# A mixture of experts in a four-layer kernel: the gather between the first pair's products, slots counted by products, two more weight buffers, and six of eight combines done two by two

## The chip, the cores and the metric

The kernel runs on one core of a Trainium2 chip. The metric is the device time of one execution in microseconds (us). A core has five engines that work side by side: TensorE (PE in the profile; its weight loads are PEld), VectorE (DVE), ScalarE (ACT), GpSimd (POOL) and SyncE (SP), which here only issues DMA transfers. Each has its own instruction order and waits for the others by semaphores.

## The reference

Four layers over 256 latent tokens and 256 context tokens, 1024 channels. Each layer mixes the tokens in three recurrent branches and ends in an expert-choice mixture; the change is in that last part alone. Each of the 16 experts takes the 32 tokens of a stream with the highest probability for it, and its result is added to those tokens, weighted by that probability:

```python
def moe_ec(h, router_w, w1, w3, w2):
    B, n, _ = h.shape
    cap = max(1, CAP_FACTOR * n // N_EXPERTS)
    probs = jax.nn.softmax((h @ router_w).astype(jnp.float32), axis=-1)
    aff, idx = lax.top_k(jnp.swapaxes(probs, 1, 2), cap)
    bidx = jnp.arange(B)[:, None, None]
    xe = h[bidx, idx]
    hid = jax.nn.silu(jnp.einsum('becd,edf->becf', xe, w1)) * jnp.einsum('becd,edf->becf', xe, w3)
    ye = jnp.einsum('becf,efd->becd', hid, w2) * aff[..., None].astype(h.dtype)
    return jnp.zeros_like(h).at[bidx, idx].add(ye)
...
        x = x + mod_x[5][:, None] * moe_ec(h2x, router_w[l], moe_w1[l], moe_w3[l], moe_w2[l])
        if not last:
            ctx = ctx + mod_c[2][:, None] * merge_branches((a_c, b_c, m_c), gate_c, w_branch[l], w_out[l])
            h2c = modulate(rmsnorm(ctx, norm2_g[l]), mod_c[3], mod_c[4])
            ctx = ctx + mod_c[5][:, None] * moe_ec(h2c, router_w[l], moe_w1[l], moe_w3[l], moe_w2[l])
```

Layers 0 to 2 send both streams (512 tokens) through the experts, the last layer only the latent tokens. All weights of all experts are read in every layer, 402 MB in the whole kernel.

## The kernel before

**Route and slots.** The expert stage starts when the probabilities of the tokens stand as rows, one row for each expert and stream. Four rounds of max and match_replace mark the 32 chosen tokens (`sel`, 0 or 1). A scan on VectorE (L1599) counts them along a row, so that a chosen token gets its slot 1 to 32, and a multiplication (L1601) puts 0 at the others. Two transposes (L1604) turn this by token, and a comparison with 1 to 32 (L1614) makes `OH`, a 0/1 matrix from tokens to slots: for each of four tiles of 128 tokens, 16 experts x 32 slots.

**Gather.** `gather(eh)` multiplies the tokens, split into a high and a low part (`tok`), with `OH`: for each of eight channel tiles kk and each stream s, four products (L1630) into a bank `bi` (context) or `ai` (latent), then one eviction that applies scale and shift, on VectorE for the context stream (L1637), on ScalarE for the latent stream (L1635). `gather(0)` serves experts 0 to 7 and stands ahead of all expert products, `gather(1)` serves 8 to 15 and stands behind the w1 and w3 products of the first pair.

**Pairs.** The 16 experts go in eight pairs `pr_`. An expert has 64 slots, 32 of each stream, so that the two experts q = 0, 1 of a pair fill 128. For each pair: w1 products into `df` or `dm`, w3 products into the other (both L1650, 32 each: the two experts' products run side by side on the two 64-column halves of the array), SiLU on ScalarE and VectorE, four transposes (L1676) and a copy to `mrawf` (L1678), then 32 w2 products (L1684) into `ac` and `bi`. The **combine** brings the result back to the tokens: `Cm` holds which slot belongs to which token, from transposes (L1664) of `OH` times the probability, `aff` the probability of each slot. ScalarE scales and rounds (L1687, `mhif`), VectorE makes the rest (L1688, `mlof`), 16 products of 512 columns (L1694) follow, and VectorE adds each of them to the residual `xT` (L1697, two operations, one for each stream).

**Loads.** `Weights` hands out the expert weights: a load of 512 KB (tile `mw`) is half of the rows of w1, w3 or w2 that a step needs for one expert. A pair has 24 loads (8 of w1, 8 of w3, 8 of w2), a layer 192. They go through `N_MW` buffers:

```python
            i, l = self.n, self.l
            self.n += 1
            e, j = 2 * (i // 24) + i % 2, i % 24 // 2
            t = self.z.mt([1024], "mw", N_MW)
```

Four of these buffers hold another matrix (`ml`) until the products of the step ahead of the experts (w_out) are done. Loads for the first pair are asked for early, in `Weights.ahead`; the loop that calls it does so 16 times, fewer than `N_PRE`. SyncE issues all loads in order over eight semaphores, so that a load also waits for the eighth one before it to land.

**What sets the order.** A scheduler at build time orders the instructions of each engine by estimated times; so the combine of one pair is threaded into the w1 products of the next.

Of the kernel before, what the change touches and what calls it, by code (L numbers as in the profile page):

```python
# [30 lines left out]
def _consts():  # L31
# [47 lines left out]
N_MW = 22  # L79
# [27 lines left out]
N_PRE = 18  # L107
# [46 lines left out]
def tile_backbone(ctx: ExitStack, tc: tile.TileContext, A, out, dbg=None, depth=DEPTH):  # L154
# [1370 lines left out]
    def moe(z, l, P, last, rt, sums, W):  # L1525
# [92 lines left out]
        if last:  # L1618
            for xg in xe:
                gp.memset(xg[:, :, :, 0:32], 0.0)  # L1620

        def gather(eh):
            for kk in range(8):
                g, k = kk // 4, kk % 4
                for s in range(st0, 2):
# [6 lines left out]
                    o, pv = xe[g][:, k, 8 * eh:8 * eh + 8, 32 * s:32 * s + 32], ps.rearrange("p (e c) -> p e c", e=8)  # L1632
                    sc, sh = der[:, 1, kk, s:s + 1], mod[:, 24 + kk, s:s + 1]
                    if s:
                        se.activation(o, pv, AF.Identity, scale=sc, bias=sh)  # L1635
# [4 lines left out]
        for pr_ in range(8):  # L1640
            e0 = 2 * pr_
            ab = []
            for wn in ("w1", "w3"):
# [9 lines left out]
            if pr_ == 0:  # L1653
                gather(1)

            Ow = w2k("ada").rearrange("p (t e c) -> p t e c", t=4, e=2)
            gp.memset(Ow, 0.0)  # L1657
            for t in range(tl, 4):
                s = t // 2
                ve.tensor_tensor(Ow[:, t, :, 32 * s:32 * s + 32], OHf[:, t, e0 * 32:e0 * 32 + 64].rearrange("p (e c) -> p e c", e=2),  # L1660
                                 lg[:, t, e0:e0 + 2, None].to_broadcast([128, 2, 32]), ALU.mult)
# [102 lines left out]
```

## Time and profile before

| | |
|---|---|
| time, median of 3 runs | 5003.71 us (5001.26 to 5008.22) |
| the profiled execution | 5006.14 us, its span 5004.4 us |
| TensorE busy | 4513.4 us, 90% of the span |
| VectorE / ScalarE / GpSimd busy | 60% / 29% / 28% |
| data read from HBM | 795.81 MB |
| loads of expert weights | 768 of 512 KB |

In the trace the first w1 products of layers 0 to 3 start at 1056, 2326, 3601 and 4742 us, and the last pair's w2 products end near 1304, 2574, 3849 and 4980. A row of a timeline gives the start, the length, the engine, the line, the operation with its tiles (output <- inputs), how many instructions it holds, and in brackets the idle time before it and what ended it.

### The profile page before, as it was taken

What the parts mean: (1) busy time and instruction counts of PE and PEld (TensorE: products, weight loads), DVE (VectorE), ACT (ScalarE), POOL (GpSimd) and SP (SyncE); (2) the same over time, 40 slices, a digit from 0 to 9 for tenths busy, and PEclk for the clock granted to TensorE, in tenths of its full rate; (3) what the DMA queues carried; (4) which work ended last, traced back from release to release, by engine and by line L of the source; (5) the groups of instructions that cost most, each with busy time, mean ns of one, the idle gap of its engine ahead of it and who ended that gap; (6) DMA issues with size and microseconds to landing.
All of it is one profiled execution on the core that took longest, in us unless ns stands there. A gap on an engine that the chain in (4) does not pass through costs nothing.

```text
span 5004.4 us, 84862 instructions
## 1 busy us (share of the span) xinstructions
PE 4513.4 (90%) x31882; PEld 2934.2 (59%) x31882; DVE 2998.8 (60%) x8123; ACT 1470.0 (29%) x2932; POOL 1405.1 (28%) x1815
## 2 busy tenths in 40 slices
PE   7999999999889999989998999998998888887798
PEld 4666666653466666665336666666633666675533
DVE  4786757533477766663347777656333677776322
ACT  3333323220233332322023333332301433332211
POOL 3332323410243233232014333233300433332400
PEclk9999999999999999999999999999999899898899
DMA  5433446679532434457963244345697233333598
GB/s 219 119 112 110 119 148 202 234 262 393 214 106 65 126 106 125 156 191 257 394 258 110 63 119 112 101 150 167 234 390 289 77 83 84 86 88 107 198 392 315
DMA packets 684010, 886.03 MB, mean 177 GB/s; under 512 B 337072, under 2 KB 361264, under 8 KB 670800
## 3 DMA queue, kind: packets, MB, share of 16 engines
q1 hardware_dynamic: 683600, 880.60, 52.7%
q8 instruction: 252, 4.13, 0.3%
q14 instruction: 158, 1.29, 0.1%
HBM read 795.81 MB, written 84.63 MB: 176 GB/s over the span
## 4 chain that ended last, share of the span: by engine, by line
PE 50%; DVE 20%; DMA 6%; issue 4%; ACT 3%; POOL 2%; SPq 0%; DVEq 0%; ACTq 0%; POOLq 0%
PE df L393 9%; PE dm L393 8%; PE df L1650 5%; PE ai L211 5%; PE bi L211 5%; PE dm L1650 4%; PE bi L1694 3%; PE ac L211 2%; PE ac L1684 2%; PE bi L1684 2%; DMA t<-gates 2%; DVE cv L1037 2%; DMA mw<-in_w_dram 1%; DVE sv L428 1%; POOL wlo L367 1%
## 5 line engine op out<-in xcount | busy, mean ns | idle before, releaser
L367 POOL TENSOR_TENSOR wlo<-wraw,whi 128x512 fp32r<-128x512 f32 x696 | 942.6, 1359 | 1934.3 <-ACT whi L366 1708.0
L393 PE MATMUL df<-big,whi 128*128 128x512 f32 (+1 forms) x2944 | 892.0, 384 | 0.0
L393 PE MATMUL dm<-big,whi 128*128 128x512 f32 (+1 forms) x2368 | 740.1, 392 | 1.1 <-DVE big L367 1.1
L393 PE MATMUL df<-big,wlo 128*128 128x512 f32 (+1 forms) x1536 | 650.8, 424 | 70.3 <-POOL wlo L367 23.2
L366 ACT CAST whi<-wraw 128x512 fp32r<-128x512 f32 x696 | 426.5, 617 | 870.6 <-PE df L393 442.4
L393 PEld LDWEIGHTS df<-big,whi 128*128 128x128 f32 x2944 | 567.5, 201 | 90.8 <-issue 3.7
L393 PE MATMUL dm<-big,wlo 128*128 128x512 f32 (+1 forms) x1248 | 528.5, 424 | 57.0 <-POOL wlo L367 18.6
L393 PEld LDWEIGHTS dm<-big,whi 128*128 128x128 f32 x2368 | 458.9, 198 | 85.4 <-DVE big L367 2.8
L393 PEld LDWEIGHTS df<-big,wlo 128*128 128x128 f32 x1536 | 306.7, 200 | 197.0 <-issue 97.1
L393 PEld LDWEIGHTS dm<-big,wlo 128*128 128x128 f32 x1248 | 247.1, 198 | 164.9 <-issue 71.9
L1650 PE MATMUL df<-mw,big 128*64 128x512 f32 x1024 | 302.2, 610 | 0.0
L1037 DVE SCALAR_TENSOR_TENSOR cv<-cv,par,cv 128x255 f32<-128x255 f32 (+3 forms) x472 | 249.0, 539 | 42.6 <-ACT cv L1034 38.8
L1697 DVE SCALAR_TENSOR_TENSOR big<-bi,der,big 128x256 f32<-128x256 f32 x448 | 191.8, 478 | 120.3 <-PE bi L1694 119.9
L1650 PE MATMUL dm<-mw,big 128*64 128x512 f32 x1024 | 255.7, 594 | 2.1 <-DMA mw<-in_w_dram 1.9
L1657 POOL MEMSET mada<- 128x512 f32 x32 | 16.8, 525 | 800.7 <-PE bi L1694 350.4
L722 DVE SCALAR_TENSOR_TENSOR big<-cv,muc,big 128x252 f32<-128x252 f32 (+2 forms) x280 | 156.6, 581 | 33.2 <-ACT big L719 31.8
L1650 PEld LDWEIGHTS dm<-mw,big 128*64 128x64 f32 x1024 | 80.8, 137 | 152.5 <-issue 136.7
L1688 DVE SCALAR_TENSOR_TENSOR mlof<-ac,aff,mhif 128x512 fp32r<-128x512 f32 x32 | 24.0, 750 | 212.3 <-ACT mhif L1687 212.3
L211 PE MATMUL ai<-AR,BK 64*128 64x128 f32 (+1 forms) x1024 | 124.0, 320 | 29.8 <-POOL BK L905 12.3
L1684 PE MATMUL ac<-mw,mrawf 128*64 128x512 f32 x512 | 139.6, 600 | 9.9 <-ACT mrawf L1678 9.9
L1694 PEld LDWEIGHTS bi<-mada,mhif 128*128 128x128 f32 x256 | 48.0, 187 | 155.1 <-issue 82.7
L1684 PE MATMUL bi<-mw,mrawf 128*64 128x512 f32 x512 | 138.1, 592 | 0.0
(514 smaller groups left out, 7871.8 us busy)
## 6 DMA issues: line engine op xcount, KB each, us to landing
mw<-in_w_dram SPq DMA_DIRECT2D x768, 512.0 KB, 10.4
wraw<-in_w_in_dram SPq DMA_DIRECT2D x536, 256.0 KB, 2.8
adaw<-in_ada_w_dram SPq DMA_DIRECT2D x96, 1024.0 KB, 6.3
gates<-gt SPq DMA_DIRECT2D x114, 256.0 KB, 3.4
wraw<-in_w_branch_dram SPq DMA_DIRECT2D x96, 256.0 KB, 2.7
t<-gates SPq DMA_DIRECT2D x85, 256.0 KB, 3.7
TU<-zoai SPq DMA_DIRECT2D x128, 128.0 KB, 3.1
wraw<-in_w_out_dram SPq DMA_DIRECT2D x64, 256.0 KB, 5.1
```

What stands on the lines that cost most here:

```text
L211: mm(o, a, b, **kw)
L366: se.copy(dst_hi, src)
L367: eng.tensor_tensor(dst_lo, src, dst_hi.bitcast(F32), ALU.subtract)
L393: mm(ps[:, c0:c1], a[:, k % 4, :], bk[:, c0:c1], start=(n == 0), stop=(n == 3 * nk - 1))
L428: ve.tensor_tensor(tv, Xb[:, j + 1:, j:j + 1].to_broadcast(sh), Xb[:, j:j + 1, 0:j].to_broadcast(sh), ALU.mult)
L722: ve.scalar_tensor_tensor(dst, src, muc[:, 1 + q, rb:rb + 1], dst, ALU.mult, ALU.add)
L1037: ve.scalar_tensor_tensor(dst, src, cw[:, cb, t:t + 1], dst, ALU.mult, ALU.add)
L1650: mm(ps[64 * q:64 * q + 64, :], xe[k // 4][:, k % 4, e0 + q, :], wt[q][:, k2 * 512:(k2 + 1) * 512], start=(k == 0), stop=(k == 7))
L1684: mm(py[hf][64 * q:64 * q + 64, :], hT[:, kk, 64 * q:64 * q + 64], wt[q][:, hf * 512:(hf + 1) * 512], start=(kk == 0), stop=(kk == 3))
L1688: ve.scalar_tensor_tensor(yl[hf], py[hf], aff, yh[hf].bitcast(F32), ALU.mult, ALU.subtract)
L1694: mm(pcb[:, n], y[db // 4][:, db % 4 * 128:(db % 4 + 1) * 128], Cm[:, n], start=y is yh, stop=y is yl)
L1697: ve.scalar_tensor_tensor(xT[:, db, cs_], pcb[:, cs_], der[:, 3, db, s:s + 1], xT[:, db, cs_], ALU.mult, ALU.add)
```

## The change

Four things change, in `route_begin`'s expert part and in two constants.

1. The slots: `sel` is transposed first, and the count along the tokens is made by three products with a triangular matrix (`mf_0`) and a matrix of ones.
2. `gather(0)` is cut: channel tiles 0 and 1 ahead of the first product, the others between the steps of the first pair's w1 products. An eviction becomes two, each for every other pair, because the place of the streams in a pair's 64 slots now depends on the pair's parity (`s ^ r_`).
3. `N_MW` 22 becomes 24, `N_PRE` 18 becomes 20.
4. Pairs 0 to 5 are combined two by two. With the streams swapped in odd pairs, a tile of 128 rows can hold one stream of two pairs: after an even pair four copies, each masked to one stream by `af`, put its w2 products into `ys`; after an odd pair four operations add its own. `ys` is then split into a high part (ScalarE) and a low part (VectorE for one half of the channels, GpSimd for the other), and one combine of 32 products of 256 columns serves both pairs. Pairs 6 and 7 are combined alone, as before.

```diff
-N_MW = 22
+N_MW = 24
...
-        sel, slot = z.mt([256], "sel"), z.mt([256], "slot")
-        ve.tensor_scalar(sel[lp], wk[lp], -1.0, None, ALU.is_equal)
-        ve.tensor_tensor_scan(slot[lp], C["ones"][lp, 0:1].to_broadcast([64 - 32 * st0, 256]), sel[lp], 0.0, ALU.mult, ALU.add)
-
-        ve.tensor_tensor(slot[lp], slot[lp], sel[lp], ALU.mult)
+        ve.tensor_scalar(wk[lp], wk[lp], -1.0, None, ALU.is_equal)
...
+        ve.tensor_copy(sel[:, :, sv], pst[:, 0:128].rearrange("p (q e) -> p q e", q=2)[:, :, sv])
+
+        pst = z.psm()
+        mm(pst[:, 32 * st0:64], C["mf_0"], sel[:, 0, sv], start=True, stop=True)
+        mm(pst[:, 64 + 32 * st0:128], C["ones"], sel[:, 0, sv], start=True, stop=False)
+        mm(pst[:, 64 + 32 * st0:128], C["mf_0"], sel[:, 1, sv], start=False, stop=True)
+        ve.tensor_tensor(stm[:, :, sv], pst[:, 0:128].rearrange("p (q e) -> p q e", q=2)[:, :, sv], sel[:, :, sv], ALU.mult)
...
-        gather(0)
+                    for r_ in range(2):
+                        o = xv[:, :, r_, :, 32 * (s ^ r_):32 * (s ^ r_) + 32]
+                        if s:
+                            se.activation(o, pv[:, :, r_], AF.Identity, scale=sc, bias=sh)
+                        else:
+                            ve.tensor_scalar(o, pv[:, :, r_], sc, sh, ALU.mult, ALU.add)
+        gather(0, range(2))
...
+                    if pr_ == 0 and wn == "w1" and kk < 3:
+                        gather(0, range(2 * kk + 2, 2 * kk + 4))
                     wt = [W.take() for q in range(2)]
...
+            if r_ == 0:
+                ys = [[w2k("rawm") for hf in range(2)], [z.mt([512], "ys", 2) for hf in range(2)]]
             for hf in range(2):
-                se.activation(yh[hf], py[hf], AF.Copy, scale=aff)
-                ve.scalar_tensor_tensor(yl[hf], py[hf], aff, yh[hf].bitcast(F32), ALU.mult, ALU.subtract)
...
+                for s in range(st0, 2):
+                    if r_ == 0:
+                        se.activation(ys[s][hf], py[hf], AF.Copy, scale=af[:, 0, s:s + 1])
+                    else:
+                        ve.scalar_tensor_tensor(ys[s][hf], py[hf], af[:, 1, s:s + 1], ys[s][hf], ALU.mult, ALU.add)
+            if r_ == 0:
+                continue
+            yh, yl = [[[w2k(x + f, F32R) for _ in range(2)] for f in "fm"] for x in ("hi", "lo")]
+            for hf in range(2):
+                for s in range(st0, 2):
+                    split(yh[s][hf], yl[s][hf], ys[s][hf], (ve, gp)[hf])
             for db in range(8):
                 pcb = psum("bi")
-                for y in (yh, yl):
-                    mm(pcb[:, n], y[db // 4][:, db % 4 * 128:(db % 4 + 1) * 128], Cm[:, n], start=y is yh, stop=y is yl)
                 for s in range(st0, 2):
                     cs_ = slice(s * 256, (s + 1) * 256)
+                    for y in (yh, yl):
+                        mm(pcb[:, cs_], y[s][db // 4][:, db % 4 * 128:(db % 4 + 1) * 128], Cm[:, cs_], start=y is yh, stop=y is yl)
```

TensorE's order in layer 0 before, at the end of `gather(0)` (L1630; `ai` is the bank, `OH` and the parts of a token tile the inputs) and the first w1 products (L1650, into `df`, `mw` the weights, `big` the gathered tokens):

```order
L1630 MATMUL ai_10598<-OH_10497,mada_10460 128x256
L1630 MATMUL ai_10598<-OH_10497,mada_10461 128x256
L1630 MATMUL ai_10598<-OH_10497,ssq_10471 128x256
L1630 MATMUL ai_10598<-OH_10497,gt_10472 128x256
L1650 MATMUL df_10604<-mw_9996,big_10506 64x512
L1650 MATMUL df_10604<-mw_9998,big_10506 64x512
L1650 MATMUL df_10604<-mw_9996,big_10506 64x512
L1650 MATMUL df_10604<-mw_9998,big_10506 64x512
```

After the change, where the gather is L1634 and the expert products L1660:

```order
L1634 MATMUL ai_10546<-OH_10499,mhim_10416 128x256
L1634 MATMUL ai_10546<-OH_10499,mlom_10417 128x256
L1634 MATMUL ai_10546<-OH_10499,mhif_10427 128x256
L1634 MATMUL ai_10546<-OH_10499,mlof_10428 128x256
L1660 MATMUL df_10538<-mw_9996,big_10508 64x512
L1634 MATMUL bi_10539<-OH_10499,mhim_10394 128x256
L1634 MATMUL bi_10539<-OH_10499,mlom_10395 128x256
L1634 MATMUL bi_10539<-OH_10499,mhif_10405 128x256
L1634 MATMUL bi_10539<-OH_10499,mlof_10406 128x256
L1634 MATMUL bi_10553<-OH_10499,mhim_10394 128x256
L1634 MATMUL bi_10553<-OH_10499,mlom_10395 128x256
```

The first product now stands behind the gather of the first channel tiles and stands alone; the gather of the next ones follows it, and the other products of its step come behind that.

TensorE's order in layer 0 before, where the w2 products of pair 2 (L1684) end and its combine (L1694) meets pair 3's w1 products:

```order
L1684 MATMUL bi_11112<-mw_11137,mrawf_11109 64x512
L1684 MATMUL ac_11111<-mw_11139,mrawf_11109 64x512
L1684 MATMUL bi_11112<-mw_11139,mrawf_11109 64x512
L1664 MATMUL ai_11265<-cst,mada_11259 128x128
L1694 MATMUL bi_11153<-mada_11095,mhif_11145 128x512
L1650 MATMUL df_11193<-mw_11194,big_10506 64x512
L1694 MATMUL bi_11153<-mada_11095,mlof_11147 128x512
L1694 MATMUL bi_11158<-mada_11095,mhif_11145 128x512
L1694 MATMUL bi_11158<-mada_11095,mlof_11147 128x512
L1650 MATMUL df_11193<-mw_11196,big_10506 64x512
L1650 MATMUL df_11193<-mw_11194,big_10506 64x512
```

After the change, at the same place (w2 products L1715), no combine follows:

```order
L1715 MATMUL ac_11134<-mw_11160,mrawf_11132 64x512
L1715 MATMUL ac_11134<-mw_11162,mrawf_11132 64x512
L1715 MATMUL bi_11135<-mw_11160,mrawf_11132 64x512
L1715 MATMUL bi_11135<-mw_11162,mrawf_11132 64x512
L1660 MATMUL df_11176<-mw_11177,big_10508 64x512
L1660 MATMUL df_11176<-mw_11179,big_10508 64x512
L1660 MATMUL df_11176<-mw_11177,big_10508 64x512
L1660 MATMUL df_11176<-mw_11179,big_10508 64x512
L1660 MATMUL df_11176<-mw_11185,big_10508 64x512
L1660 MATMUL df_11176<-mw_11187,big_10508 64x512
```

The w1 products of pair 3 stand in one block, two halves side by side. Behind pair 1 the combine of pairs 0 and 1 (L1753) is threaded into pair 2's w1 products after the change:

```order
L1715 MATMUL bi_10924<-mw_10949,mrawf_10921 64x512
L1715 MATMUL bi_10924<-mw_10951,mrawf_10921 64x512
L1660 MATMUL df_11033<-mw_11036,big_10508 64x512
L1660 MATMUL df_11033<-mw_11042,big_10508 64x512
L1753 MATMUL bi_10977<-mada_10782,mhif_10961 128x256
L1660 MATMUL df_11033<-mw_11044,big_10508 64x512
L1660 MATMUL df_11033<-mw_11042,big_10508 64x512
L1660 MATMUL df_11033<-mw_11044,big_10508 64x512
L1660 MATMUL df_11033<-mw_11050,big_10509 64x512
L1753 MATMUL bi_10984<-mada_10782,mhif_10961 128x256
L1753 MATMUL bi_10977<-mada_10782,mlof_10965 128x256
```

Six w1 products stand ahead of the first product with a low part (`mlof`).

SyncE's order in layer 0 before the change, with the waits of each issue, where the w2 loads of pair 0 (L1492) meet pair 1's w1 loads (L1490); `DMAHW` is the landing of an earlier load, `PE` a buffer that TensorE frees, and adaw (and wraw, later in the stage) are loads of the next layer's other weights:

```order
L1492 DMA mw_10763<-in_w_dram 128x1024 [waits DMAHW2_49]
L1492 DMA mw_10765<-in_w_dram 128x1024 [waits DMAHW3_49]
L1492 DMA mw_10771<-in_w_dram 128x1024 [waits DMAHW4_49,PE_49]
L1492 DMA mw_10773<-in_w_dram 128x1024 [waits DMAHW5_49,PE_49]
L1492 DMA mw_10779<-in_w_dram 128x1024 [waits DMAHW6_49,PE_49]
L1492 DMA mw_10781<-in_w_dram 128x1024 [waits DMAHW7_49,DVE_49,PE_49]
L306 DMA adaw_13612<-in_ada_w_dram 128x2048 [waits DMAHW0_49,PE_49]
L1492 DMA mw_10787<-in_w_dram 128x1024 [waits DMAHW1_49,PE_49]
L1492 DMA mw_10789<-in_w_dram 128x1024 [waits DMAHW2_49,PE_49]
L1490 DMA mw_10844<-in_w_dram 128x2x512 [waits DMAHW3_49,PE_49]
```

After the change (L1493, L1491, adaw L307):

```order
L1493 DMA mw_10805<-in_w_dram 128x1024 [waits DMAHW2_49]
L1493 DMA mw_10807<-in_w_dram 128x1024 [waits DMAHW3_49]
L1493 DMA mw_10813<-in_w_dram 128x1024 [waits DMAHW4_49]
L1493 DMA mw_10815<-in_w_dram 128x1024 [waits DMAHW5_49]
L1493 DMA mw_10821<-in_w_dram 128x1024 [waits DMAHW6_49,PE_49]
L1493 DMA mw_10823<-in_w_dram 128x1024 [waits DMAHW7_49,PE_49]
L1493 DMA mw_10829<-in_w_dram 128x1024 [waits DMAHW0_49,PE_49]
L1493 DMA mw_10831<-in_w_dram 128x1024 [waits DMAHW1_49,DVE_49,PE_49]
L307 DMA adaw_13589<-in_ada_w_dram 128x2048 [waits DMAHW2_49,PE_49]
L1491 DMA mw_10846<-in_w_dram 128x2x512 [waits DMAHW3_49,PE_49]
```

Four loads instead of two go out without a wait for TensorE, and all eight w2 loads stand ahead of the adaw load.

## Rows read from the trace of the kernel before

**Rows 1.** Page, 40 slices: GB/s moved, slice by slice.

```profile
GB/s 219 119 112 110 119 148 202 234 262 393 214 106 65 126 106 125 156 191 257 394 258 110 63 119 112 101 150 167 234 390 289 77 83 84 86 88 107 198 392 315
```

**Rows 2.** Windows view: stretch, length, busy by engine, PEclk, DMA share, GB/s.

```profile
core 0: us, PE busy (x) PEld busy (x) DVE busy (x) ACT busy (x) POOL busy (x), PEclk, DMA share, GB/s
...
1080.00:1099.40 19.40, 19.40 (x80) 6.33 (x80) 9.17 (x23) 1.90 (x3) 0.12 (x1) 1.00 0.94 355
1161.25:1192.97 31.72, 29.89 (x123) 10.55 (x121) 11.44 (x26) 2.45 (x4) 0.53 (x1) 1.00 1.04 394
4800.00:4880.00 80.00, 74.75 (x336) 27.83 (x334) 22.39 (x48) 7.46 (x12) 1.58 (x3) 1.00 1.04 395
```

**Rows 3.** Timeline of SyncE's DMA issues, layer 0 and layer 3: start, length, count.

```profile
1058.10 0.80 SPq L1492 DMA_DIRECT2D mw<-in_w_dram  x2
...
1271.36 9.78 SPq L1492 DMA_DIRECT2D mw<-in_w_dram  x8
1282.10 1.62 SPq L374 DMA_DIRECT2D wraw<-in_w_in_dram  x2
...
4958.77 9.78 SPq L1492 DMA_DIRECT2D mw<-in_w_dram  x8
```

**Rows 4.** Page, DMA issues: count, KB each, us to landing.

```profile
mw<-in_w_dram SPq DMA_DIRECT2D x768, 512.0 KB, 10.4
```

**Rows 5.** Timeline of TensorE, end of layer 0's w2 products, then layer 3's.

```profile
1303.62 1.08 PE L1684 MATMUL bi<-mw,mrawf 128*64 128x512 f32 x4
...
4968.20 1.93 PE L1650 MATMUL dm<-mw,big 128*64 128x512 f32 x6 [0.26 <-DMA mw<-in_w_dram]
...
4978.73 0.59 PE L1684 MATMUL bi<-mw,mrawf 128*64 128x512 f32 x1
```

**Rows 6.** Timeline of TensorE, one steady pair of layer 0 [idle before].

```profile
1192.97 7.45 PE L1650 MATMUL dm<-mw,big 128*64 128x512 f32 x31
...
1210.44 0.50 PE L1694 MATMUL bi<-mada,mhif 128*128 128x512 f32 x1 [0.76 <-ACT mhif L1687]
1210.87 1.07 PE L1650 MATMUL df<-mw,big 128*64 128x512 f32 x2
...
1224.64 1.88 PE L1650 MATMUL dm<-mw,big 128*64 128x512 f32 x7
```

**Rows 7.** Timeline of TensorE, layer 0, between pairs 0 and 1.

```profile
1087.74 0.50 PE L1694 MATMUL bi<-mada,mhif 128*128 128x512 f32 x1
...
1099.39 7.45 PE L1650 MATMUL dm<-mw,big 128*64 128x512 f32 x31
```

**Rows 8.** Timeline of VectorE, layer 0, from the selection to the slots.

```profile
1040.43 1.63 DVE L1599 TENSOR_TENSOR_SCAN slot<-cst,sel 64x256 f32<-64x256 f32 x1
1042.10 1.30 DVE L1601 TENSOR_TENSOR slot<-slot,sel 64x256 f32<-64x256 f32 x1
1043.97 0.29 DVE L1607 COPY stm<-ai 128x128 f32<-128x128 f32 x1 [0.57 <-PE ai L1604]
```

**Rows 9.** Timeline of TensorE, layer 0: first gather, w1 and w2 products.

```profile
1044.87 0.58 PE L1630 MATMUL bi<-OH,mhim 128*128 128x256 f32 x1 [0.94 <-DVE OH L1614]
...
1056.14 7.09 PE L1650 MATMUL df<-mw,big 128*64 128x512 f32 x32
...
1080.74 1.03 PE L1684 MATMUL ac<-mw,mrawf 128*64 128x512 f32 x4
```

**Rows 10.** Groups by line: count, min/median/max ns, first and last start.

```profile
L1635 ACT ACTIVATE big<-ai,mod,der x64: 562/565/567, 1047.6 to 4768.6; 128x256 f32<-128x256 f32 x64
...
L1687 ACT ACTIVATE mhif<-ac,aff x32: 687/688/689, 1087.0 to 4979.5; 128x512 fp32r<-128x512 f32 x32
...
L1688 DVE SCALAR_TENSOR_TENSOR mlof<-ac,aff,mhif x32: 741/751/752, 1087.7 to 4980.2; 128x512 fp32r<-128x512 f32 x32
```

**Rows 11.** Windows view, layer 0: first and later gather products.

```profile
1044.80:1049.40 4.60, 4.53 (x20) 4.34 (x20) 3.36 (x10) 1.13 (x2) 0.00 (x0) 0.50 0.00 0
1050.70:1056.10 5.40, 5.40 (x45) 5.27 (x44) 2.97 (x6) 2.26 (x4) 0.00 (x0) 1.00 0.00 0
```

More of the change, by code (lines that the diff above doesn't have):

```diff
@@ L106 @@
 AM0, AMS = 800.0, 0.0
-N_PRE = 18
+N_PRE = 20
 AD, AD0 = 180.0, 30.0
@@ L1619, in moe, with gather @@
             for xg in xe:
-                gp.memset(xg[:, :, :, 0:32], 0.0)
-        def gather(eh):
-            for kk in range(8):
+                for r_ in range(2):
+                    gp.memset(xg.rearrange("p k (a r q) c -> p k a r q c", r=2, q=2)[:, :, :, r_, :, 32 * r_:32 * r_ + 32], 0.0)
+        def gather(eh, kks):
+            for kk in kks:
                 g, k = kk // 4, kk % 4
@@ L1653, in moe @@
             if pr_ == 0:
[L1654 to L1661, printed above, removed]
-            pc = z.psm()
-            for t in range(tl, 4):
-                te.transpose(pc[:, t * 128:(t + 1) * 128], Ow[:, t].rearrange("p e c -> p (e c)"), ident)
@@ new lines, in moe @@
+            if pr_ >= 6:
+                yh, yl = [w2k("hif", F32R) for _ in range(2)], [w2k("lof", F32R) for _ in range(2)]
+                for hf in range(2):
+                    se.activation(yh[hf], py[hf], AF.Copy, scale=aff[:, 0:1])
+                    ve.scalar_tensor_tensor(yl[hf], py[hf], aff[:, 0:1], yh[hf].bitcast(F32), ALU.mult, ALU.subtract)
+                if pr_ == 7:
+                    X["ss"] = psum("dm")
+                for db in range(8):
+                    pcb = psum("bi")
+                    for y in (yh, yl):
+                        mm(pcb[:, n], y[db // 4][:, db % 4 * 128:(db % 4 + 1) * 128], Cm[:, n], start=y is yh, stop=y is yl)
+                    for s in range(st0, 2):
+                        cs_ = slice(s * 256, (s + 1) * 256)
+                        ve.scalar_tensor_tensor(xT[:, db, cs_], pcb[:, cs_], der[:, 3, db, s:s + 1], xT[:, db, cs_], ALU.mult, ALU.add)
+                    if pr_ == 7:
+                        sums.add_all(db, xT[:, db], X["ss"])
+                continue
@@ new lines, in moe @@
+            if r_ == 0:
+                ys = [[w2k("rawm") for hf in range(2)], [z.mt([512], "ys", 2) for hf in range(2)]]
+            for hf in range(2):
+                for s in range(st0, 2):
+                    if r_ == 0:
[3 more added lines that the diff above has]
+            if r_ == 0:
+                continue
```

63 lines of the change are left out of this document (45 added, 18 removed).

## Prediction

> **What bounds the kernel now.** I read the 40 slices of the page first. The data rate stands at 390 or more in four places, one for each layer [rows 1]: these are the expert stages, and the change touches nothing else. So the question is what bounds an expert stage. The windows of the second view [rows 2] say that the sixteen DMA engines are full there: from pair 1 on the share is 1.04 at 394 GB/s, in layer 0 (one full pair stands for the four like it) and in layer 3. A load of 524,288 B then takes 524,288 / 394,000 = 1.33 us, and a pair's 24 loads 31.9 us, as long as a pair takes on TensorE (dm to dm, 1192.97 to 1224.64, 31.67 us [rows 6]). The two run at one pace because a load waits for a buffer that TensorE frees.
>
> Which of them would give way? In layers 0 to 2 the loads lie ahead. A layer has 768 / 4 = 192 [rows 4]. SyncE issues 170 of them (192 less the 22 buffers) after the first products have freed a buffer, the first at 1058.10, the last at 1271.36 + 9.78 = 1281.1 [rows 3]; with the median landing of 10.4 us [rows 4] the last one lands near 1291.5, and near 1289 if the queue is shorter by then. The group of w2 products that uses it starts at 1303.62 [rows 5]; four products are two side-by-side pairs of 0.43 (below), so w2 ends at 1304.5. The loads are 12 us ahead: in these layers TensorE ends last. In layer 3, with half the tokens, it is the other way round: TensorE stops for a load in the last pair's w3 products (idle 0.26, ended by DMA [rows 5]), and the last w2 products at 4978.73 come with the last landing, 4968.5 + 10.4 [rows 3 to 5]. Layer 3 is bound by the loads already.
>
> **Combine of six pairs two by two.** Now every pair's combine (16 products of 512 columns) is threaded into the next pair's w1 products. Alone, 32 products take 7.45 less a tail of 0.57, 6.88 us, since two 64-column halves run side by side, 0.43 a pair (the first row of [rows 6]). With the combine between them it takes from 1210.44 to 1224.64, 14.20 us, after an idle 0.76; a side-by-side pair that is broken up costs about 1.0 (1.07 for two records [rows 6]). So a pair boundary without a combine saves 14.20 + 0.76 - 6.88 = 8.1 us. It is gone after pairs 0, 2 and 4. After pair 0 the stretch is 1087.74 to 1099.39 [rows 7], 11.65 us with 26 products left, 26 x 0.215 = 5.6: 6.05 saved. Sum 6.05 + 2 x 8.1 = 22.2 us for each of layers 0 to 2. The combine after pairs 1, 3 and 5 has 32 products of 256 columns, the columns of one old combine, so it keeps its price.
>
> What it adds: on ScalarE four copies like L1687 (0.69 [rows 10]) after an even pair. They free the two accumulators that TensorE needs only at the next w2 products, over 13 us later: hidden. After an odd pair VectorE runs four operations like L1688 (0.75 [rows 10], 3.0 us), and the splits come on top, before a low half can be multiplied; now it is one copy and one such operation. Behind the waiting product stand w1 products on TensorE. The order after pair 1 puts six of them ahead of the first low half, which cover most of the wait. Bounds: 0 (all covered) and 3.0 us (nothing covered); I take 0.8, nearer the first, since the first two w1 products stand alone at about 1.0 each. Left: 22.2 - 2.4 = 19.8 us. TensorE alone would end the layer's w2 products at 1304.5 - 19.8 = 1284.7.
>
> **Slots counted by products.** The scan (1.63) and the multiplication (1.30) with a 0.04 gap go: 2.97 us [rows 8]. In their place come three small products and a multiplication out of PSUM; nearest is the copy that stands there now, 0.29 with 0.57 of waiting for TensorE before it [rows 8], and I allow 0.5 for the products: 1.35. Saved 1.6 us; bounds 0.5 and 2.5.
>
> **Gather between the first products.** Nothing is removed: the same gather products stand before and between the first w1 products, so the first of these moves from 1056.14 to about 1048.5, and w3 hardly moves. The order breaks up one or two side-by-side pairs (0.6 each), and every switch costs a bit: +1.5 us, bounds 0 and 3. The evictions become twice as many with half the elements; one of 256 takes 0.565 [rows 10], so two halves take at most 1.13 beside eight gather products of 0.12 (0.96 us [rows 11]): hidden but for the bound just given. So the first w2 products, 1080.74 now [rows 9], stay where they are within 1.5 us.
>
> What the earlier products could give is earlier loads: the first buffer comes free some 5 us before 1058.10. But w1 and w3 of pair 0 free only 16 buffers, and the next ones come with the w2 products at 1080.74; 16 loads need 16 x 1.33 = 21 us, which 1058.1 already leaves. The head start is spent waiting in the second gather, ahead of the w2 products.
>
> **Two more buffers.** All 24 loads of pair 0 are then issued before its first product (on SyncE the two extra ones pass ahead of an adaw load). At 1080.74 two more loads are done, 2 x 1.33 = 2.7 us for the end of the loads. The rate is 355 GB/s in 1080 to 1099 against 394 later [rows 2]: 19.4 x (1 - 355/394) = 1.9 us that unbroken w1 products, which free buffers faster, may give back.
>
> **The sum.** In layers 0 to 2 the loads now end last. They end at 1291.5 - 2.7 = 1288.8 (at best 1289 - 2.7 - 1.9 = 1284.4). The last two buffers serve two groups of products, 1.7 us more: 1290.5 (1286). The gain is 1304.5 - 1290.5 = 14.0, up to 18.5; I take 15, nearer the first since the 10.4 is measured. TensorE's own bound (19.8) lies 5 us beyond. Three layers: 45. Layer 3, where the loads end last already, gains the 2.7 and about the 1.6 of the slots, since its first pair starts earlier by that: 4.2. Together 49: 5006.1 (the profiled execution, 1.7 over its span) - 49 = 4957. The median of the three runs is 2.4 lower: **4955 us**. Its own range: 12 to 18.5 a layer and 3 to 5 for layer 3, so 39 to 60 us: 4944 to 4965.
>
> **Rivals.** A, the loads don't bind: if buffers come free sooner and the queue never runs dry, TensorE's 19.8 to 22.2 is gained in full, 59 to 67 + 4: 4933 to 4940, about 4938. For it: the bound at best (18.5) is near. Against: the share is 1.04 already, and no window has more than 395. Chance 0.12.
>
> B, the longer chain after odd pairs is in the open: at the bound of 3.0 us or more, with the splits on GpSimd late for the second half, each of the three combines loses 3 to 5 us, so that 22.2 shrinks to 7 to 13 a layer and TensorE stays last. 21 to 39 + 4: 4961 to 4979, about 4970. For it: the idle 0.76 of today comes from a chain of a single copy. Against: w1 products are there to fill it. Chance 0.14.
>
> C, slower: TensorE's clock falls. After waits like the 0.94 before the first gather product [rows 9] it was granted 0.50, the lower of its two levels (1.2 GHz), and 20 gather products took 4.60 us; at 1.00 (2.4 GHz) 45 took 5.40 [rows 11]. The change makes TensorE wait for loads in pairs 5 to 7. A pair without waits is 3 x 6.88 + 3 = 23.6 us; at the lower level about 45, which is 13 over the 31.9 of its loads. Three such pairs in four layers are +156, less the 49: 5110. It ends slower from somewhat over one such pair a layer (15 / 13). Against: layer 3 waits for loads today, and its window shows 1.00 with TensorE busy 74.75 of 80 us [rows 2]. Chance 0.04.
> The Trainium skill (TensorE: Matmul & The Clock Gate, HAM oscillation) tells of a kernel whose clock falls in each wait for a transfer. The rows of layer 3 show such waits without it.
>
> D, the loads bind already: if a load took longer than 1.33 us, the end of the loads would be the end of the layer today, and only the 2.7 a layer and the 1.6 of layer 3 would be gained, 12 us: 4991. Against: 394 and 395 GB/s [rows 2] and the 12 us by which the last load is early. Chance 0.01.
> The Trainium skill (DMA: Bandwidth & Descriptors, Where 436 GB/s comes from) has transfers from HBM bound by a core's share of it, about 358 GB/s. An estimate by that page is 1.46 us a load, and 154 loads from 1080 would end at 1305; the trace disagrees in every full pair.
>
> E, no change: what follows takes the gain back. The next layer's first weights go out right behind the last expert load, at 1282.10 now [rows 3], 22 us before the w2 products end; that lead falls to about 11. Chance 0.04.
>
> **How the numbers follow.** Forecast 0.65 (4944 to 4965), A 0.12, B 0.14, C 0.04, D 0.01, E 0.04. The range 4938 to 4978 takes in nearly all of B and the edge of A. 0.2% is 10 us, about what a measurement of this kernel tells from no change. Faster by more than that: forecast, A, B and D, 0.92; within 0.04 (E); slower 0.04 (C).
>
> **What would show it.** Right: the w1 products after pairs 0, 2 and 4 in one block of 7 us; waits for loads on TensorE in pairs 5 to 7 of layers 0 to 2, at a clock of 1.00; a DMA share of 1.04 from pair 1 to the last load; the first product of layer 0 near 1048.5 and its first w2 products near 1081; the last group of w2 products near 1289. Wrong: no wait for loads at the end (A), TensorE idle for over 3 us at the combine after odd pairs (B), a clock under 1 in the pairs (C), the last expert load as late as now (D).

## Result and the profile after

The changed kernel takes 4949.97 us (median of four runs, 4939.53 to 4968.46), the kernel before 5005.8 us beside it: ratio 0.9894, 95% interval 0.9863 to 0.9924. It is faster, by some 53 us (1.1%) by the ratio and 56 by the two medians; 4955 us was forecast. The profiled execution took 4948.79 us, its span is 4946.3 us.

The single execution is a blunt measure: the changed kernel's runs differ by 29 us. The expert stages, read between two fixed instructions, are not. From the start of the first gather product to the end of the last w2 product, in us by layer, and the distance from the end of the last expert load's issue in layer 0 to the end of its w2 products:

| kernel | layer 0 | layer 1 | layer 2 | layer 3 | last issue to end, layer 0 |
|---|---|---|---|---|---|
| before | 259.8 | 259.9 | 258.2 | 241.1 | 23.6 |
| after | 245.6 | 244.5 | 244.7 | 238.6 | 11.8 |
| difference | -14.3 | -15.4 | -13.6 | -2.5 | |

In the kernel before, layer 3 alone had a distance of 11.8: the last issue row of [rows 3] ends at 4968.55, the last w2 products at 4979.29 + 1.02 = 4980.31.

```profile
4979.29 1.02 PE L1684 MATMUL bi<-mw,mrawf 128*64 128x512 f32 x2
```

In layer 0 before, TensorE hardly waited for an expert load (waits view, 1060 to 1304 us: in all 0.7 us, twice, 0.4 the longest):

```profile
PEld df L1650 <- DMA mw<-in_w_dram: 0.7, 2, 0.4
```

The page's slices still have one hump of the data rate for each layer, as [rows 1]:

```profile
GB/s 218 122 102 113 126 138 194 217 268 394 259 110 63 118 115 117 163 174 264 394 292 111 66 119 112 107 151 162 246 382 302 86 79 88 84 88 107 213 392 310
```

The windows view after the change (columns as [rows 2]) shows the same saturation from pair 1 on, in front of it a stretch with a share of 0.74, and a clock of 1.00 in all three; the first gather products ahead of them still ran at 0.50:

```profile
1047.00:1052.00 5.00, 4.45 (x20) 4.33 (x20) 4.17 (x13) 1.44 (x4) 0.00 (x0) 0.50 0.00 0
1084.00:1090.00 6.00, 6.00 (x30) 2.01 (x28) 1.76 (x13) 0.00 (x0) 0.00 (x0) 1.00 0.74 258
1100.00:1182.00 82.00, 77.85 (x366) 29.83 (x364) 31.57 (x73) 10.31 (x17) 7.09 (x5) 1.00 1.04 392
1182.00:1290.00 108.00, 99.42 (x418) 36.95 (x415) 28.50 (x56) 10.89 (x18) 3.81 (x3) 1.00 1.04 395
```

TensorE's timeline after, layer 0: the first gather product (L1634), the first w1 product (L1660), the first w2 products (L1715), pair 3's w1 products, the three waits in the combine behind pair 3 (L1753), waits for loads in pair 5's w3 products, and the end:

```profile
1047.55 0.58 PE L1634 MATMUL bi<-OH,mhim 128*128 128x256 f32 x1 [0.84 <-DVE OH L1617]
...
1052.31 1.10 PE L1660 MATMUL df<-mw,big 128*64 128x512 f32 x2
...
1084.03 1.03 PE L1715 MATMUL ac<-mw,mrawf 128*64 128x512 f32 x4
...
1143.32 7.04 PE L1660 MATMUL df<-mw,big 128*64 128x512 f32 x32
...
1168.05 0.38 PE L1753 MATMUL bi<-mada,mhif 128*128 128x256 f32 x1 [0.75 <-ACT mhif L367]
...
1169.98 0.39 PE L1753 MATMUL bi<-mada,mlof 128*128 128x256 f32 x1 [0.53 <-DVE mlof L368]
...
1171.66 0.39 PE L1753 MATMUL bi<-mada,mlom 128*128 128x256 f32 x1 [0.95 <-DVE mlom L368]
...
1208.95 2.43 PE L1660 MATMUL dm<-mw,big 128*64 128x512 f32 x8 [0.22 <-DMA mw<-in_w_dram]
1211.66 2.44 PE L1660 MATMUL dm<-mw,big 128*64 128x512 f32 x8 [0.28 <-DMA mw<-in_w_dram]
1214.37 2.43 PE L1660 MATMUL dm<-mw,big 128*64 128x512 f32 x8 [0.27 <-DMA mw<-in_w_dram]
...
1292.10 1.02 PE L1715 MATMUL bi<-mw,mrawf 128*64 128x512 f32 x2
```

The block of w1 products in 7.04 us is what the combine used to break up: [rows 6] had 14.20 us there. The kernel's loops issue 16 products for a pair's w1, and the trace counts 32: it has two records for each, so the counts of 32 for w1, w3 and w2 are counts of records, x4 is two products side by side and x2 one alone. In pair 5 eight records, the products of two loads, start every 2.71 us: the pace of the loads, twice 1.33, where the unbroken block needs 1.7. SyncE's issues after, to be held against [rows 3]:

```profile
1056.09 18.98 SPq L1491 DMA_DIRECT2D mw<-in_w_dram  x16
...
1271.48 9.80 SPq L1493 DMA_DIRECT2D mw<-in_w_dram  x8
1282.24 1.61 SPq L375 DMA_DIRECT2D wraw<-in_w_in_dram  x2
```

The last issue ends at 1281.28, 233.7 us after the first gather product (1047.55); before it was 236.3. With the page's median landing of 10.5 us the last load lands at 1291.8, among the last pair's w2 products, which end at 1293.12 and take 8.1 us instead of the 7.1 of the kernel before. The waits view, layer 0 from 1182 us (pair 4's w3 products) to the end, has these waits of TensorE's weight loads for an expert load of w1 or w3 (total, times, longest); 12 of the 14, 8.8 us, are in pair 5:

```profile
PEld dm L1660 <- DMA mw<-in_w_dram: 6.6, 9, 1.2
PEld df L1660 <- DMA mw<-in_w_dram: 3.3, 5, 1.2
```

The way from the selection to the slots on VectorE, against [rows 8]:

```profile
1043.20 1.37 DVE L1598 TENSOR_SCALAR lT<-lT 64x256 f32<-64x256 f32 x1
1045.00 0.29 DVE L1604 COPY sel<-ai 128x128 f32<-128x128 f32 x1 [0.43 <-PE ai L1601]
1046.74 0.29 DVE L1610 TENSOR_TENSOR stm<-ai,sel 128x128 f32<-128x128 f32 x1 [1.45 <-PE ai L1609]
1047.07 2.77 DVE L1617 TENSOR_TENSOR OH<-cst,stm 128x256 fp32r<-128x256 f32 x8
```

From the end of the is_equal operation (L1598, 1044.57) to the first comparison that makes OH (1047.07) it is 2.50 us; before, from 1040.39 to 1044.30, 3.91. In layers 1 and 2 it is 2.8 and 2.9 after against 3.9 and 4.0 before. In layer 3, with one stream, it is the other way round. Before, then after:

```profile
4736.34 0.28 DVE L1598 TENSOR_SCALAR sel<-wk 32x256 f32<-32x256 f32 x1
...
4738.62 1.43 DVE L1614 TENSOR_TENSOR OH<-cst,stm 128x256 fp32r<-128x256 f32 x4
```

```profile
4679.32 0.28 DVE L1598 TENSOR_SCALAR lT<-lT 32x256 f32<-32x256 f32 x1
...
4681.98 0.22 DVE L1610 TENSOR_TENSOR stm<-ai,sel 128x64 f32<-128x64 f32 x1 [1.58 <-PE ai L1609]
4682.24 1.43 DVE L1617 TENSOR_TENSOR OH<-cst,stm 128x256 fp32r<-128x256 f32 x4
```

That is 2.00 us before and 2.64 after: there the products cost 0.6 us instead of saving any.

### The profile page after: what moved, and what is told of

Read it like the earlier page. It is cut to its first block, busy times and chain, and to the rows that moved or that the text cites. A ratio compares the mean times of both kernels' runs of the same rounds, so it can differ in the third digit from the quotient of the medians.

```text
span 4946.3 us, 84721 instructions
## 1 busy us (share of the span) xinstructions
PE 4446.9 (90%) x31816; PEld 2922.0 (59%) x31816; DVE 2938.0 (59%) x8032; ACT 1504.4 (30%) x3032; POOL 1422.9 (29%) x1814
## 4 chain that ended last, share of the span: by engine, by line
PE 47%; DVE 20%; DMA 8%; issue 4%; ACT 3%; POOL 2%; SPq 0%; ACTq 0%; POOLq 0%; DVEq 0%
PE df L394 9%; PE dm L394 8%; PE ai L212 5%; PE bi L212 5%; PE df L1660 4%; DMA mw<-in_w_dram 3%; PE dm L1660 3%; PE ac L212 2%; PE ac L1715 2%; PE bi L1715 2%; DVE cv L1038 2%; POOL wlo L368 2%; DVE sv L429 1%; DVE Y L430 1%; PE bi L1753 1%
## 5 line engine op out<-in xcount | busy, mean ns | idle before, releaser
L1660 PE MATMUL df<-mw,big 128*64 128x512 f32 x1024 | 286.2, 605 | 2.6 <-DMA mw<-in_w_dram 2.5
L1660 PE MATMUL dm<-mw,big 128*64 128x512 f32 x1024 | 264.8, 597 | 7.0 <-DMA mw<-in_w_dram 6.9
L1660 PEld LDWEIGHTS dm<-mw,big 128*64 128x64 f32 x1024 | 80.4, 136 | 167.6 <-issue 120.9
L723 DVE SCALAR_TENSOR_TENSOR big<-cv,muc,big 128x252 f32<-128x252 f32 (+2 forms) x280 | 157.6, 585 | 32.4 <-ACT big L720 31.1
L1702 DVE SCALAR_TENSOR_TENSOR t<-t,df 128x512 f32<-128x512 f32 x32 | 22.0, 687 | 246.1 <-ACT t L1701 246.1
L368 POOL TENSOR_TENSOR mlof<-mrawm,mhif 128x512 fp32r<-128x512 f32 x9 | 14.4, 1598 | 509.0 <-ACT mhif L367 357.5
L1715 PE MATMUL ac<-mw,mrawf 128*64 128x512 f32 x512 | 150.0, 602 | 10.9 <-ACT mrawf L1709 10.9
L212 PE MATMUL ai<-AR,BK 64*128 64x128 f32 (+1 forms) x1024 | 124.1, 320 | 30.3 <-POOL BK L906 13.6
L1715 PE MATMUL bi<-mw,mrawf 128*64 128x512 f32 x512 | 148.5, 592 | 0.0
L1660 PEld LDWEIGHTS df<-mw,big 128*64 128x64 f32 x1024 | 74.1, 136 | 120.7 <-issue 87.5
L1704 DVE TENSOR_TENSOR t<-t,dm 128x512 f32<-128x512 f32 x32 | 22.0, 687 | 198.4 <-PE dm L1660 198.4
## 6 DMA issues: line engine op xcount, KB each, us to landing
mw<-in_w_dram SPq DMA_DIRECT2D x768, 512.0 KB, 10.5
```

Of the source, the lines that this page charges most:

```text
L212: mm(o, a, b, **kw)
L368: eng.tensor_tensor(dst_lo, src, dst_hi.bitcast(F32), ALU.subtract)
L723: ve.scalar_tensor_tensor(dst, src, muc[:, 1 + q, rb:rb + 1], dst, ALU.mult, ALU.add)
L1660: mm(ps[64 * q:64 * q + 64, :], xe[k // 4][:, k % 4, e0 + q, :], wt[q][:, k2 * 512:(k2 + 1) * 512], start=(k == 0), stop=(k == 7))
L1702: ve.scalar_tensor_tensor(th, th, 1.0, ab[0], ALU.add, ALU.mult)
L1715: mm(py[hf][64 * q:64 * q + 64, :], hT[:, kk, 64 * q:64 * q + 64], wt[q][:, hf * 512:(hf + 1) * 512], start=(kk == 0), stop=(kk == 3))
```

## Experiments

The theory: in layers 0 to 2 TensorE ended last before, the two-by-two combine takes its surplus away, and now the loads end last. The rivals: TensorE's own longer chain ends last after the change too; or the loads set the pace before already, and the gain is that of the buffers and the earlier start. All stretches stand in one table (us, as above; the ratio is to the kernel before, with its interval):

| run | ratio | layer 0 | layer 1 | layer 2 | layer 3 | last issue to end |
|---|---|---|---|---|---|---|
| after once more | 0.9889 (0.9871 to 0.9906) | 244.4 | 245.0 | 244.5 | 238.5 | 11.8 |
| after, w2 loads halved | 0.9778 (0.9753 to 0.9802) | 231.3 | 231.3 | 230.0 | 213.4 | 24.6 |
| before, w2 loads halved | 0.9917 (0.9888 to 0.9947) | 252.0 | 251.6 | 249.9 | 229.0 | 24.6 |
| after, 22 buffers | 0.9940 (0.9920 to 0.9961) | 247.6 | 249.4 | 248.8 | 240.2 | 11.8 |
| before, 24 buffers | 0.9984 (0.9971 to 0.9998) | 258.5 | 259.1 | 257.0 | 238.8 | 25.0 |
| after, each pair combined alone | 0.9976 (0.9962 to 0.9989) | 258.1 | 258.4 | 256.6 | 238.9 | 25.4 |
| after, first gather whole | 0.9906 (0.9889 to 0.9923) | 246.8 | 246.2 | 245.5 | 238.6 | 12.3 |
| after, scan again | 0.9928 (0.9902 to 0.9953) | 246.4 | 246.0 | 245.8 | 238.6 | 11.8 |
| after, w1 and w3 in turn | 0.9923 (0.9897 to 0.9949) | 245.5 | 245.0 | 246.8 | 236.9 | 11.8 |
| after, half of the second gather later | 0.9886 (0.9863 to 0.9910) | 243.8 | 242.2 | 241.4 | 237.0 | 11.8 |
| both of the last two | 0.9872 (0.9854 to 0.9890) | 241.5 | 242.7 | 241.1 | 237.3 | 11.8 |

The last column sorts the kernels. Wherever two-by-two combining and full loads meet, the w2 products of layer 0 end 11.8 us behind the last issue (12.3 once): one landing of 10.5 and the last products. Elsewhere they end 23.6 to 25.4 us behind it.

**The changed kernel once more.**

> The changed kernel itself once more, on the chip of the next three, as their measure. Its stretches from first gather to last w2 product should come out at 244.5 to 245.6 in layers 0 to 2 and 238.6 in layer 3 again, and its ratio to the kernel before near 0.989.

It came out at 244.4 to 245.0 and 238.5: the stretches repeat within 1.2 us, and differences of 2 us between kernels can be read from them, where times can't tell them.

**The loads made shorter.**

```diff
-                sy.dma_start(t, A["w2"][l, e, (j - 8) * 128:(j - 7) * 128, :])
+                sy.dma_start(t[:, 0:512], A["w2"][l, e, (j - 8) * 128:(j - 7) * 128, 0:512])
...
-                        mm(py[hf][64 * q:64 * q + 64, :], hT[:, kk, 64 * q:64 * q + 64], wt[q][:, hf * 512:(hf + 1) * 512], start=(kk == 0), stop=(kk == 3))
+                        mm(py[hf][64 * q:64 * q + 64, :], hT[:, kk, 64 * q:64 * q + 64], wt[q][:, 0:512], start=(kk == 0), stop=(kk == 3))
```

> The changed kernel with the w2 loads cut to half: each brings 512 of 1024 columns (256 KB), and the products of the second half of the channels use the first half's columns again, so that part of w2 is left out; products and their order stay. A pair then loads 20 units of 512 KB, 26.6 us instead of 31.9. Theory (the loads end last): layers 0 to 2 become bound by TensorE and the stretch from the first gather product to the last w2 product falls by another 4 to 6 us from 244.5, to about 239.5; layer 3 falls from 238.6 to about 203 (pairs of 23.8 and 27 us as its first ones). Sum about 15 + 35 = 50 below the changed kernel, near 4900 us, and no waits for loads in layers 0 to 2. Rival (TensorE's own chain ends last in layers 0 to 2): those stretches stay within 1 us of 244.5, only layer 3 falls, near 4915.

Against the changed kernel once more, layers 0 to 2 fell by 13.1, 13.7 and 14.5 us instead of 4 to 6, layer 3 by 25 instead of 35. The order of the products did not stay, as the next run shows for the kernel before. The waits for loads at the end of layer 0 are gone but for one (waits view of the run with halved loads, 1180 to 1278 us):

```profile
PEld df L1660 <- DMA mw<-in_w_dram: 0.4, 1, 0.4
```

This speaks against the rival that TensorE's chain ends last after the change; the other order alone might give 8 us (next run), and 13 to 14.5 are more than that. The waits in pair 5 and the constant 11.8 us of the table say the same without a change of the loads. 231.3 is 28.5 us under the kernel before, where the prediction had 19.8 for TensorE alone.

> The kernel before with the same halved w2 loads (the same part of w2 left out). Theory (TensorE ends last in layers 0 to 2, loads in layer 3): the stretch from first gather to last w2 product stays within 2 us of 259.5 in layers 0 to 2, layer 3 falls by about 8 us from 241.1 (its pairs go from 29 to 32 us back to the 28.3 of the ones in the middle); about 4998 us. Rival (the loads set the pace before as well): layers 0 to 2 fall by 10 us or more each, 4970 or less.

Here neither came true: layers 0 to 2 fell by 8 us (layer 3 by 12 instead of 8), though TensorE's weight loads hardly waited for an expert load in either kernel (in layer 0 0.7 us before, 3.6 here). The scheduler orders by estimated times, and shorter loads gave TensorE another order: of the some 21,200 products of the whole program, a line-by-line comparison of the two built orders finds some 6,300 differing lines, and some 6,100 between the changed kernel and its halved run. TensorE's timeline of this run at a place like that of [rows 6], the end of the w2 products and the combine, which follows without the 0.76 of idle time:

```profile
1203.67 1.03 PE L1684 MATMUL bi<-mw,mrawf 128*64 128x512 f32 x4
1204.70 0.50 PE L1694 MATMUL bi<-mada,mhif 128*128 128x512 f32 x1
1205.13 1.07 PE L1650 MATMUL df<-mw,big 128*64 128x512 f32 x2
...
1206.56 1.08 PE L1650 MATMUL df<-mw,big 128*64 128x512 f32 x4
```

The steady pairs, w2 to w2, take 30.0 to 30.7 us instead of 31.7. So an experiment that changes a size here changes the order as well, and both halved runs mix the two. That the order made the 8 us is argued from the missing waits; it was not tried alone. What compares like with like are the two halved runs, in both of which TensorE ends 24.6 us behind the last issue: 252.0 to 231.3, 251.6 to 231.3 and 249.9 to 230.0, that is 20.7, 20.3 and 19.9 us, close to the 19.8.

**The buffers.** `N_MW` alone, 22 in the changed kernel and 24 in the kernel before.

> The changed kernel with 22 weight buffers. Theory (loads end last, so each load that isn't done ahead costs 1.33 us): +2.7 us in each of the four stretches, about +11 us, near 4961. Rival (the buffers are no part of it): within 1 us in each stretch, 0.

Against the changed kernel once more the stretches grew by 3.2, 4.3, 4.3 and 1.7 us, 13.6 in all (10.8 expected); the time grew by more, to 4976.18 us, of which the last section speaks. `N_PRE` was not varied.

> The kernel before with 24 weight buffers and nothing else. Theory: in layers 0 to 2 TensorE ends last, so nothing is gained there (stretches within 1 us of 259.5); layer 3, bound by the loads, falls by 2.7 us from 241.1: about 5003, the same as before. Rival (the two buffers give 2.7 us in every layer): -11 us.

1.3, 0.8, 1.2 and 2.4 us less than in the kernel before: as expected in layer 3, and about 1 us, hardly more than two runs of one kernel differ by, where TensorE ends last. The same two buffers are worth 12 us in layers 0 to 2 once the loads bind there, 3 us where they don't.

**The combine alone.**

```diff
-            if pr_ < 6 and pr_ % 2 == 0:
+            if pr_ < 0:
...
-            elif pr_ >= 6:
+            else:
...
-            if pr_ >= 6:
+            if pr_ >= 0:
```

> The changed kernel with every pair combined alone as before (slots by products, split gather and 24 buffers stay). Theory (TensorE's broken w1 products were what ended last before, and two-by-two combining is what removed them): layers 0 to 2 go back to 257 to 259 us, layer 3 stays within 1 us of 238.6; about +40 us over the changed kernel. Rival (the gain came from earlier loads through the split gather and the buffers): layers 0 to 2 stay below 250.

258.1, 258.4 and 256.6, the stretches of the kernel before with 24 buffers (258.5, 259.1, 257.0): split gather and slots add nothing to a stretch that TensorE ends. Over the changed kernel once more the four stretches are 39.6 us longer, as expected (the time by 47 us, by the ratios some 43). Its timelines, SyncE's last loads and TensorE's last w2 products in layer 0, show the lead that the loads keep:

```profile
1268.03 9.78 SPq L1493 DMA_DIRECT2D mw<-in_w_dram  x8
...
1302.10 1.08 PE L1715 MATMUL bi<-mw,mrawf 128*64 128x512 f32 x4
```

The rival that the gain came from buffers and the earlier start falls.

**The gather whole.** `gather(0, range(8))` ahead of the products, nothing between them.

> The changed kernel with the first gather whole again ahead of the first product. Theory (the loads' head start is spent waiting in the second gather): the first product moves from +4.5 to about +11.5 us after the first gather product, but the stretches stay within 1.5 us of 244.9 and 238.6; 0 to +5 us in all. Rival (loads are what ends last, so a later restart costs its whole delay): +4 to +7 us a layer, +16 to +28 us.

The scheduler still put one product early; the next stand 12.5 us behind the first gather product (1047.57), and the loads go on 13.7 us behind it instead of 8.5 (8.0 in the changed kernel once more):

```profile
1053.11 1.58 PE L1658 MATMUL df<-mw,big 128*64 128x512 f32 x2
1060.12 2.37 PE L1658 MATMUL df<-mw,big 128*64 128x512 f32 x10
...
1061.24 14.82 SPq L1491 DMA_DIRECT2D mw<-in_w_dram  x16
```

Of the 5 us by which the split moves the restart in layer 0, 2.4 reach the end of the stretch, more than the 1.5 allowed; in layers 1 to 3 the stretches are 1.2, 0.9 and 0.1 us longer. Most of the head start is spent waiting, as forecast.

**The scan again.**

> The changed kernel with the slots counted by the scan and the multiplication again. Theory: on VectorE the way from the end of the selection (the is_equal operation) to the first comparison that makes OH goes from 2.5 to 2.8 us back to 3.9, in each layer; the stretches behind stay within 1 us; +5 us in all, less than the measurement tells. Rival (the products' way is no shorter, since each step waits for TensorE): no difference in that way.

In layer 0 the way is 3.9 us again (1042.51 to 1046.41) against 2.5 and 2.8 in the two runs of the changed kernel. In layers 1 and 2 it is 3.9 and 4.0, in layer 3 2.0, where the changed kernel takes 2.6: the theory, which had the scan slower in each layer, fails there. The stretches came out up to 2 us longer (2.0, 0.9, 1.2 and 0.1) instead of within 1, at the edge of what they tell.

**A step further.** If the loads end last, what frees buffers earlier shortens the stage. First, pair 0's w1 and w3 products and loads in turn; second, half of the second gather in pair 1:

```diff
+            if i < 16:
+                j = j // 2 + 4 * (j % 2)
...
+            two = (psd(), psd())
+            for wi, kk in ([(wi, kk) for kk in range(4) for wi in range(2)] if pr_ == 0 else [(wi, kk) for wi in range(2) for kk in range(4)]):
...
-                gather(1, range(8))
+                gather(1, range(4, 8))
...
+                    if pr_ == 1 and wi == 0:
+                        gather(1, [kk])
```

> The changed kernel with pair 0's w1 and w3 products and loads taken in turn, and nothing else. Theory (what is gained before the second gather is spent waiting in it, since pair 0 frees only 16 buffers ahead of its w2 products): the loads restart 3 us earlier, w2 products stay at +36, the stretches stay within 1.5 us of 244.6. Rival (an earlier restart counts in full): -3 us or more a layer.

Nothing is gained in layers 0 to 2 (1.1 and 2.3 us longer, 0.1 shorter), 1.6 us in layer 3. The restart did not come earlier (8.0 us behind the gather's start, as in the changed kernel once more), so the run doesn't tell the two apart.

> The changed kernel with half of the second gather moved into pair 1's w1 products, and nothing else. Theory (the w2 products of pair 0 free the buffers that the loads wait for): w2 products at +32 instead of +36, stretches 2 to 3 us shorter in layers 0 to 2. Rival (only the first restart counts, or TensorE's work in pair 1 takes it back): within 1 us.

Shorter by 0.6, 2.8, 3.1 and 1.6 us; the w2 products of pair 0 start at +33.9, +32.2 and +32.1 in layers 0 to 2 instead of +36. The theory holds in layers 1 and 2; in layer 0, where these products came only 2 us earlier, the stretch gained no more than the rival allows.

> The changed kernel with pair 0's w1 and w3 products taken in turn (its loads in that order too), so that buffers come free at 0.75 a us from the first product on, and half of the second gather moved into pair 1's w1 products, so that pair 0's w2 products start some 4 us earlier. Theory (loads end last): the DMA share between the restart and 45 us later rises from 0.66 to 0.95 towards 1.04, the loads end earlier and each layer's stretch is 4 to 7 us shorter; about -20 us, near 0.985 of the kernel before. Rival (TensorE's chain in pairs 3 to 7 ends last): 0 within 1.5 us a layer.

Shorter by 2.9, 2.3, 3.4 and 1.2 us: less than expected, 9.9 in all before rounding, and 0.9872 against 0.9889 on the same chip, with intervals that overlap. In the 45 us behind the restart the DMA share went from 0.87 to 0.93, not to 1.04. The loads of layer 0 end 2.9 us earlier (last issue 229.7 us behind the first gather product against 232.6 in the changed kernel once more), as much as the stretch is shorter, and the last w2 products end again 11.8 us behind the last issue, which ends at 1271.11:

```profile
1261.31 9.80 SPq L1495 DMA_DIRECT2D mw<-in_w_dram  x8
...
1281.92 1.02 PE L1719 MATMUL bi<-mw,mrawf 128*64 128x512 f32 x2
```

By the stretches this version beats both kernels; by the time it can't be told from the changed one. Half of the second gather alone gave 8.1 of the 9.9 us, so taking the products in turn added little.

## Why the prediction was right, step by step

- **Who ends last before.** TensorE in layers 0 to 2, the loads in layer 3: the distances of 23.6 and 11.8 us and the run with 24 buffers in the kernel before bear it out. In layer 3 the last w2 products start at 4979.29 and not at 4978.73, which changes nothing. What the step missed is that the order itself depends on the loads.
- **Combine two by two.** Forecast 6.05 + 2 x 8.1 a layer. From the first w2 products of one pair to those of the next, in layer 0, pair 0 to 1 went from 29.1 to 22.2 us (6.9), pair 2 to 3 from 32.0 to 23.0 (9.0); pair 4 to 5 from 31.7 to 29.4 only, and there the waits for loads stand. What the prediction calls 32 products are 32 records of 16 products. Its sums, made in records throughout, stand all the same, but the two records that take 1.07 us in [rows 6] are one product alone; two side by side take no longer (x4, 1.08 us, in the run with halved loads above).
- **The longer chain.** 0.8 us taken for each; the steps from pair 1 to 2, 3 to 4 and 5 to 6, which keep a combine, take 30.1, 32.3 and 32.4 us against 29.0, 31.7 and 31.7, so 1.1, 0.6 and 0.7 longer. Behind pair 3 the waits are 0.75 + 0.53 + 0.95 = 2.2 us against 0.76. Rival B's 3 to 5 did not come.
- **TensorE's own bound**, 19.8 us: with halved loads the changed kernel lies 28 us under the kernel before, but 8 of these the halved loads gave the kernel before as well; between the two halved kernels it is 20 to 21. With full loads no run shows the bound, since the loads bind earlier.
- **Slots.** Forecast 1.6, measured 1.1 to 1.4 us in layers 0 to 2, ahead of the stretch: the three products and their copy are waited for 1.45 us, not 0.5. This step failed in layer 3, the only layer whose sum counts it: [rows 8] are of a layer with two streams, and with one the old way takes 2.00 us and the new one 2.64. In layers 0 to 2 the sum left out what the slots gave. The two errors nearly cancel, which is luck.
- **Gather.** In layer 0 the first product came 4.8 us behind the first gather product (11.3 before), the first w2 products 36.5 us behind it (35.9 before): within the 1.5 us allowed. The times named as signs (1048.5, 1081 and 1289) all came 3 to 4 us later, 2.7 of it because the stage itself began later in this execution (1047.55 against 1044.87).
- **Buffers.** 2.7 us forecast; 3.2 to 4.3 in layers 0 to 2, 1.7 in layer 3.
- **The sum.** Three layers at 15 and 4.2 for layer 3. Measured 14.3, 15.4, 13.6 and 2.5, together 45.7 before rounding, and some 3 of the slots ahead of the four stretches (1.4, 1.1, 1.1 and -0.6). The loads end last; the waits for them, forecast in pairs 5 to 7, stand almost all in pair 5 of layer 0, and in pairs 6 and 7 there are four of 1.5 us in all. The next layer's loads go out at 1282.24, 11 us ahead of the last w2 product as rival E said, and the gain was not taken back. The span shrank by 58.1; the 9 or so that are left lie outside the expert stages, where one kernel's executions differ by as much, and have no cause here. That the median came within 5 us of the forecast is partly luck: four executions lie between 4939.53 and 4968.46.
- **The clock.** It stays at 1.00 in pairs 5 to 7 in spite of waits of the weight loads of up to 1.2 us (the products themselves idled for a load 0.28 us at most), so rival C fell. The Trainium skill (TensorE: Matmul & The Clock Gate, HAM oscillation) tells of waits for transfers that let it fall; these don't.
- **The rate of the loads.** 392 and 395 GB/s, so rival D fell. The Trainium skill (DMA: Bandwidth & Descriptors, Where 436 GB/s comes from) gives 358 GB/s as the share of each of two cores in an HBM stack's bandwidth; the measurement decides, and no run here has a second core at work.

## What to carry to other kernels

Before costing what an engine saves, ask how far ahead the next limit is: here TensorE could give back some 20 us a layer, and the 12 us by which the loads were early plus about 2.7 for two buffers were what came. The distance from the last transfer's issue to the work that uses it tells which of two limits binds, and it is far steadier than the time. Where a scheduler orders by estimated times, compare the orders before a shortened transfer is read as a proof.

## What was not expected of the hardware

- Runs of the changed kernel follow the mean granted clock: it took 4939.53 us at 0.954, 4948.79 at 0.952 and 4968.46 at 0.948. In its two traces the clock is 1.00 in all four expert stages from some 6 us behind the first gather product on, and the four stretches sum to 973.3 and 972.5 us in spans of 4946.3 and 4955.9: what the two executions differ by lies outside the stretches. Over all the traces here, what lies outside goes from 3960 to 3994 us. By the ratios, the runs with 22 buffers, with the scan again and with w1 and w3 in turn lie 25, 20 and 17 us above the changed kernel once more, and their stretches explain 14, 4 and 2; which part of the rest is clock stays open.
- The same comparison on VectorE (is_equal), 64 x 256 elements, took 0.36, 1.15 and 0.34 us in layers 0 to 2 of the kernel before and 1.37, 1.13 and 1.12 after. GpSimd runs a row of operations of about 1.3 us beside it (`mrawf`, `mada`), and the comparison ends 0.18 to 0.20 us behind the start of GpSimd's next operation. In layer 0 before it ends at 1040.39, after at 1044.57 (its row after stands in the section on the result); GpSimd's next operations start at 1040.21 and 1044.38. Before, then after:

```profile
1040.03 0.36 DVE L1598 TENSOR_SCALAR sel<-wk 64x256 f32<-64x256 f32 x1
...
1040.21 1.31 POOL L1589 TENSOR_TENSOR mrawf<-t,mrawm 128x512 fp32r<-128x512 f32 x1
```

```profile
1044.38 1.31 POOL L1590 TENSOR_TENSOR mada<-t,mada 128x512 fp32r<-128x512 f32 x1
```

It is so in all 16 comparisons read from eight of the traces, 15 of them long (1.12 to 1.46 us). How long it takes is thus how much of GpSimd's running operation is left. That GpSimd holds VectorE is argued from these times; no run changes it. In layer 3 no GpSimd operation runs beside it, and it takes 0.28 us on half the rows. From the end of the last match_replace, which takes this wait in, the way to the slots went from 4.30, 5.08, 4.34 and 2.32 us to 3.90, 3.98, 4.03 and 2.95.
